# One table load at the last norm, sums of squares inside a projection, and stores and sample loads on GpSimd's queue

## The chip, the cores and the metric

The kernel runs on one core of a Trainium2 chip. A core has five engines, each with an instruction stream of its own that it works off in order: TensorE for matrix products (PE in the profile, with PEld for the load of a stationary operand), VectorE (DVE), ScalarE (ACT), GpSimd (POOL) and SyncE (SP), which here does nothing but issue DMA transfers. GpSimd can issue DMA transfers too. Engines wait for one another, and for transfers, through semaphores. The metric is device time in microseconds (us) of one execution; lower is better.

## What is computed

One inference step of a two-layer decoder for a prompt of 1024 tokens and for 8 sample tokens that share all weights. The model width is 1024. Layer 0's mixer is a gated recurrence (4 heads) beside attention into 256 memory tokens; layer 1's is stick-breaking attention beside the same kind of memory attention. Each layer has a SwiGLU network of width 2816, and an RMSNorm stands before and after each part:

```
def rmsnorm(x, g):
    return x * lax.rsqrt(jnp.mean(x * x, axis=-1, keepdims=True) + EPS) * g

def swiglu(h, w_gu, w_down):
    gate, up = jnp.split(h @ w_gu, 2, axis=-1)
    return (jax.nn.silu(gate) * up) @ w_down

for l in range(DEPTH):                 # DEPTH = 2
    hn = rmsnorm(h, g[0])
    mix = a_mixer(hn, ...) if l < N_A else b_mixer(hn, ...)     # N_A = 1
    h = h + rmsnorm(mix, g[1])
    h = h + rmsnorm(swiglu(rmsnorm(h, g[2]), w_gu[l], w_down[l]), g[3])
    if l == N_A - 1:                   # one K/V pair, shared by the layers behind it
        sb_k, sb_v = jnp.split(rmsnorm(h, g_kv) @ w_kv, 2, axis=-1)
```

A sample token attends to keys and values that come from DRAM: 256 past positions of the shared K/V, in pages that a table of page numbers points to, and 256 memory tokens per layer. Everything is float32.

## The kernel before

Activations lie with the model width on the partitions, in eight tiles of 128, and tokens along the free axis. The tokens go in two groups: g = 0 holds 512 prompt tokens, g = 1 the other 512 and the 8 sample tokens as eight last columns (520 in all, worked off as two pieces of 260). A product of two float32 operands is made from three products of rounded high and low parts, so every weight tile is fetched (L212, on SP's queue), rounded on ACT (L217) and its remainder taken on DVE (L218); the result `ws` holds four blocks of 128x128. Five raw tiles and five split tiles are in rotation. For the SwiGLU network's weights the same is done at L588, L621 and L623. PE multiplies at L231 (`proj`: one output tile, tag `mm`, two PSUM banks in rotation), L628 and L800.

The order of the work comes from generators. `weave` steps two or three of them in turn by given weights, which writes the program; a list scheduler then fixes each engine's order, and from there on every engine is in order. Places that matter here:

- `rstd_from` turns a tile of summed squares `st` into reciprocal roots. It splits it in two halves (`n`, L238 on ACT and L239 on DVE), lets PE add over the partitions with a matrix of ones (L279), and applies a logarithm (L280) and an exponential (L281) on ACT. A bank holds 512 columns, so in group 1 the loop goes round twice, for 512 columns and for the last 8, both times in the same PSUM bank `ns`, which exists once.
- `out_proj.finish` is the step behind an output projection: `rstd_from`, then `residual` for eight tiles (DVE L445 scales, L451 adds the stored residual rows that L432 fetched, L453 stores the new rows `hs` to DRAM, ACT L289 squares, DVE L290 sums), then a second `rstd_from` and `normed` (DVE L297).
- `mixer_b.heads` projects eight heads for layer 1's mixer; ACT L1490 takes a head's result from its PSUM bank. It is woven with `out_proj.finish` of the other group, twice: group 1 of layer 0 at about 930 us, and group 0 of layer 1 at about 1477 us.
- The last norm is `out_proj.finish` of group 1 in layer 1, at about 1965 us, woven with the SwiGLU network of group 0. That network's sigmoid (L646) and the norm's logarithm and exponential need different tables of ACT's activation unit, and a change of table is an instruction of its own, ACT_TABLE_LOAD, which the profile puts on the line of the activation behind it.
- The sample tokens of layer 1 (about 1520 to 1880 us) attend on DVE and ACT. `sample_scores` writes the eight queries to DRAM (`qd`, L1108), reads each back broadcast over the partitions (`b<-qd`, L1114), multiplies it into a tile of keys (L1116) and sums (L1119). The keys come by page from the shared K/V (`page_loader`, L1177, indirect DMA on GpSimd) or from the memory tokens (`mem_loader`, L1165, SP's queue). `sample_pv` scales values on ACT (L1141), and PE adds them up.

All DMAs but L1177's and those that sum gate and up weights ahead of time (L701, L703, `wsum`) are issued by SP, one after another.

Of the kernel before, what the change touches and what calls it, by code (L numbers as in the profile page):

```python
# [18 lines left out]
P = 128  # L19
# [4 lines left out]
def tile_decoder(  # L24
# [197 lines left out]

    def proj(g, W, k0, nk, m0, xt):
        w = split_w(W, k0, nk, m0)
        ps = mmp.tile([P, 2, 512], F32, tag="mm", name=nm("mm"))
        for k in range(nk):
            wh, wl = w[k]
            for wi, (wt, xi) in enumerate(((wh, 0), (wh, 1), (wl, 0))):
                for a in range(NPC[g]):
                    o = a * PW[g]  # L230
                    nc.tensor.matmul(  # L231
                        ps[:, a, : PW[g]], wt, xt[k][:, xi, o : o + PW[g]],
                        start=(k == 0 and wi == 0), stop=(k == nk - 1 and wi == 2),
                    )
        return ps

# [35 lines left out]
    def rstd_from(acc, n, inv, dst=None, bank=NS):  # L272
        r = acc if dst is None else dst
        parts = halves(acc[:, :n], *(npool.tile([P, WID], F32R, tag="n", name=nm("n"))[:, :n] for _ in range(2)))
        for o in range(0, n, 512):
            w = min(512, n - o)
            ps = bank()
            for i, p in enumerate(parts):
                nc.tensor.matmul(ps[:, :w], onesr, p[:, o : o + w], start=(i == 0), stop=(i == 1))  # L279
            nc.scalar.activation(r[:, o : o + w], ps[:, :w], AF.Ln, scale=inv, bias=epsb)  # L280
        nc.scalar.activation(r[:, :n], r[:, :n], AF.Exp, scale=-0.5)  # L281
        return r
# [139 lines left out]
    def residual(g, R, rstd, gc, store, acc=None, first=False, paced=False):  # L422
# [13 lines left out]
        for k in range(ND):  # L436
# [15 lines left out]
            if store:  # L452
                nc.sync.dma_start(hs[g][:, k, :n], R[k][:, :n])  # L453
            if acc is not None:
# [13 lines left out]
    class out_proj:  # L468
# [35 lines left out]
        def finish(self):  # L504
            g, l = self.g, self.l
            rstd = rstd_from(self.acc, NG[g], 1.0 / D)
            acc = small([P, WID], tag="st", bufs=3)
            yield from residual(g, self.R, rstd, lambda k: gcol(l, 1, k), not self.last, acc, l == 0, l == 1 and g == 0)
            r2 = rstd_from(acc, NG[g], 1.0 / D)
            yield  # L510
# [584 lines left out]

    def sample_scores(q, load, sc):
        qc = small([P, H * NB], tag="ss")
# [9 lines left out]
        qd = tc.dram_tile([NB, 512], F32, name=nm("qd"))  # L1107
        nc.sync.dma_start(qd, qt[:NB, :])  # L1108
        yield
        scv = sc.rearrange("p (k h b) -> p k h b", k=2, h=H)  # L1110
        for b in range(NB):
            kt = load(b)
            qb = B()
            nc.sync.dma_start(qb, qd[b].partition_broadcast(P))  # L1114
            with tc.issue_after(split[0].ins):
# [46 lines left out]
    def mem_loader(src, l):  # L1162
        def load(b):
            t = C()
            nc.sync.dma_start(t, src[l, b].rearrange("(k p) h d -> p k (h d)", p=P))  # L1165
            return t

        return load
# [16 lines left out]
    def mem_attn_sample(l, qm, xo):  # L1185
        HB = H * NB
        sc = small([P, 2 * HB], tag="sc", bufs=2)
        yield from sample_scores(qm, mem_loader(cache_mem_k, l), sc)
        yield
# [21 lines left out]

    def heads2(g, W, m0, xt, evac, alloc, out):
        for h in range(H):
            if h % 2 == 0:
                out.append(alloc())
            ps = proj(g, W, 0, ND, m0 + h * P, xt)
            evac(out[-1][:, h % 2, :], ps, g)
# [487 lines left out]
    class mixer_b:  # L1705
        def __init__(self, g, xt):
            self.g, self.xt, self.Qs, self.Qm = g, xt, [], []

        def heads(self):
            yield from heads2(self.g, w_in_b[0], 0, self.xt, scaled_evac, A, self.Qs)  # L1710
            yield from heads2(self.g, w_in_b[0], 4 * P, self.xt, scaled_evac, A, self.Qm)
# [164 lines left out]
    b0 = mixer_b(0, xb0)  # L1876
    weave((b0.heads(), 8), (o1.finish(), 17))
    b0.open(True)
# [18 lines left out]
    b1 = mixer_b(1, xb1)  # L1897
    weave((b1.heads(), 8), (o0.finish(), 17))
    b1.open()
# [52 lines left out]
```

## Time and profile before

| what | value |
| --- | --- |
| time, median of 3 runs | 2401.22 us (2400.32 to 2401.59) |
| the profiled execution's own time | 2400.42 us |
| its span, first to last instruction | 2398.7 us |
| PE busy | 2377.8 us, 99% |
| DVE, ACT, POOL busy | 71%, 55%, 5% |
| granted clock of TensorE | 0.999 |
| DMA | 357.60 MB in 515233 packets |

The profiled execution lies 0.80 us under the median of the three runs. Its own time is 1.7 us more than its span. An idle time in the profile is printed in brackets behind an instruction, with what released it. Waits of the queue engines (SPq, POOLq) are listed apart from those of the engines that compute.

### The profile page before, as it was taken

The page shows a single profiled execution, that of the slowest core. Times are in us where ns is not written, and L with a number is a line of the kernel's source. Part 1 is how long each engine was busy: PE and PEld are TensorE (multiplying, and loading weights), DVE is VectorE, ACT ScalarE, POOL GpSimd, SP SyncE. Part 2 cuts the span into 40 slices and gives each one's busy share as a digit, 9 for nine tenths or more (in the row PEclk, how much of TensorE's full clock was granted, in tenths as well). Part 3 has the DMA queues.
Part 4 walks back from the last instruction along what each step waited for, and adds up shares of the span by engine and source line. Part 5 has one row for each costly group of instructions (what it writes and reads, how often), then busy time and mean ns, then how long its engine had stood idle before and what let it go on. Part 6 is the DMA issues. An engine that isn't in the chain of part 4 may idle for free.

```text
span 2398.7 us, 42471 instructions
## 1 busy us (share of the span) xinstructions
PE 2377.8 (99%) x15962; PEld 2158.4 (90%) x15962; DVE 1710.1 (71%) x3197; ACT 1323.1 (55%) x2734; POOL 113.0 (5%) x187
## 2 busy tenths in 40 slices
PE   9999999999999999999999999999999999999998
PEld 7888989888889998999999989887778989999998
DVE  5867558766776677879566777877776779676866
ACT  4547544454574554667544554568557566554445
POOL 1001202101000000000001100111000000000000
PEclk9999999999999999999999999999999999999999
DMA  6454776677535447332668746544454354343442
GB/s 195 119 171 116 172 204 161 166 185 200 167 110 162 138 146 228 110 102 87 173 178 216 207 147 191 171 141 142 123 172 123 98 154 128 119 128 98 115 125 75
DMA packets 515233, 357.60 MB, mean 149 GB/s; under 512 B 20245, under 2 KB 463746, under 8 KB 515026
## 3 DMA queue, kind: packets, MB, share of 16 engines
q1 hardware_dynamic: 499154, 312.93, 44.1%
q0 software_dynamic: 15872, 41.95, 7.5%
q8 instruction: 126, 2.06, 0.4%
q14 instruction: 81, 0.66, 0.1%
HBM read 322.86 MB, written 65.49 MB: 162 GB/s over the span
## 4 chain that ended last, share of the span: by engine, by line
PE 93%; DVE 3%; ACT 2%; DMA 1%; issue 1%; SPq 0%; DVEq 0%; ACTq 0%
PE mm L231 42%; PE q L628 18%; PE q L800 12%; PE q L554 4%; PE mm L1253 2%; PE s L1434 1%; PE s L1069 1%; PE s L1050 1%; PE s L1614 1%; PE s L1657 1%; PE mm L986 1%; PE mm L1013 1%; PE q L832 1%; PE s L554 1%; PE s L1646 1%
## 5 line engine op out<-in xcount | busy, mean ns | idle before, releaser
L231 PE MATMUL mm<-x,ws 128*128 128x512 f32 (+1 forms) x5016 | 924.3, 342 | 4.1 <-ACT b L1640 2.2
L231 PEld LDWEIGHTS mm<-x,ws 128*128 128x128 f32 x5016 | 775.1, 188 | 115.5 <-ACT b L1640 2.6
L217 ACT CAST ws<-w 128x512 fp32r<-128x512 f32 x596 | 346.1, 584 | 396.9 <-PE mm L231 230.6
L218 DVE TENSOR_TENSOR ws<-w,ws 128x512 fp32r<-128x512 f32 x596 | 379.4, 644 | 225.0 <-ACT ws L217 217.0
L800 PE MATMUL q<-m,ws 128*128 128x260 f32 (+1 forms) x2496 | 303.9, 283 | 0.1
L800 PEld LDWEIGHTS q<-m,ws 128*128 128x128 f32 x2496 | 300.0, 188 | 0.9 <-ACT m L238 0.3
L628 PE MATMUL q<-y,ws 128*128 128x260 f32 (+1 forms) x1920 | 249.3, 284 | 0.0
L628 PEld LDWEIGHTS q<-y,ws 128*128 128x128 f32 x1920 | 237.7, 188 | 0.9 <-ACT q L640 0.2
L628 PE MATMUL q<-x,ws 128*128 128x260 f32 (+1 forms) x1668 | 219.8, 283 | 1.3 <-DVE ws L623 0.7
L628 PEld LDWEIGHTS q<-x,ws 128*128 128x128 f32 x1668 | 207.8, 188 | 2.2 <-DVE ws L623 1.1
L231 PE MATMUL mm<-m,ws 128*128 128x512 f32 x768 | 187.0, 397 | 0.0
L621 ACT CAST ws<-w 128x512 fp32r<-128x512 f32 x206 | 125.0, 619 | 97.1 <-PE q L800 30.7
L623 DVE TENSOR_TENSOR ws<-w,ws 128x512 fp32r<-128x512 f32 x206 | 139.2, 687 | 45.5 <-ACT ws L621 41.7
L231 PEld LDWEIGHTS mm<-m,ws 128*128 128x128 f32 x768 | 142.7, 188 | 32.0
L809 DVE TENSOR_TENSOR r<-r,q 128x260 f32<-128x260 f32 (+1 forms) x160 | 60.5, 419 | 48.7 <-PE q L800 48.3
L554 PE MATMUL q<-x,ws 128*128 128x260 f32 (+1 forms) x720 | 87.0, 282 | 0.0
L554 PEld LDWEIGHTS q<-x,ws 128*128 128x128 f32 x720 | 86.3, 188 | 0.2
L621 ACT CAST ws<-b 128x512 fp32r<-128x512 f32 x82 | 50.6, 620 | 42.4 <-PE q L800 13.4
L238 ACT CAST m<-t 128x512 fp32r<-128x512 f32 (+1 forms) x88 | 54.7, 621 | 33.3 <-DVE t L873 15.8
L239 DVE TENSOR_TENSOR m<-t,m 128x512 fp32r<-128x512 f32 (+1 forms) x88 | 60.7, 690 | 14.6 <-ACT m L238 13.7
L623 DVE TENSOR_TENSOR ws<-b,ws 128x512 fp32r<-128x512 f32 x82 | 56.3, 687 | 20.1 <-ACT ws L621 19.4
L290 DVE TENSOR_TENSOR st<-st,n 128x512 f32<-128x512 f32 (+1 forms) x91 | 62.1, 689 | 3.4 <-ACT n L289 1.9
(431 smaller groups left out, 3113.7 us busy)
## 6 DMA issues: line engine op xcount, KB each, us to landing
w<-in_w_gu SPq DMA_DIRECT2D x275, 256.0 KB, 3.3
w<-in_w_down SPq DMA_DIRECT2D x160, 256.0 KB, 3.0
wsum<-in_w_gu POOLq DMA_DIRECT2D x48, 512.0 KB, 6.3
w<-in_w_in_a SPq DMA_DIRECT2D x80, 256.0 KB, 3.3
w<-in_w_o SPq DMA_DIRECT2D x64, 256.0 KB, 3.0
w<-wsum SPq DMA_DIRECT2D x61, 256.0 KB, 3.6
b<-in_w_gu SPq DMA_DIRECT2D x39, 256.0 KB, 3.8
b<-wsum SPq DMA_DIRECT2D x39, 256.0 KB, 3.0
```

The costliest lines, as they stand in the source:

```text
L217: nc.scalar.copy(ws[:, 0, :n, :], raw[:, :n, :])
L218: split[0] = nc.vector.tensor_sub(ws[:, 1, :n, :], raw[:, :n, :], ws[:, 0, :n, :].bitcast(F32))
L231: nc.tensor.matmul(ps[:, a, : PW[g]], wt, xt[k][:, xi, o : o + PW[g]], start=(k == 0 and wi == 0), stop=(k == nk - 1 and wi == 2),)
L238: nc.scalar.copy(dst[0], src)
L239: nc.vector.tensor_sub(dst[1], src, dst[0].bitcast(F32))
L290: nc.vector.tensor_add(acc[:, :n], acc[:, :n], t[:, :n])
L554: ins = nc.tensor.matmul(pp[a][:, :h], wt, xt[k][:, xi, a * h : (a + 1) * h], start=(k == 0 and wi == 0), stop=(k == ND - 1 and wi == 2),)
L621: nc.scalar.copy(w[:, 0, :], src)
L623: split[0] = nc.vector.tensor_sub(w[:, 1, :], src, w[:, 0, :].bitcast(F32))
L628: nc.tensor.matmul(ps[:, :h], w[:, wj, k * P : (k + 1) * P], x[:, xi, :], start=(first and k == 0 and wi == 0), stop=(k == 3 and wi == 2), ...
L800: nc.tensor.matmul(pp[a][:, :h], wt, mids[k][:, xi, a * h : (a + 1) * h], start=(k == 0 and wi == 0), stop=(k == nf - 1 and wi == 2),)
L809: nc.vector.tensor_add(d, d, pp[a][:, :h])
```

## The change

It has five parts.

1. In `rstd_from` the last 8 columns of group 1 get a PSUM bank of another pool (`S()`), and all matrix products with ones are written ahead of the logarithms.
2. `heads2` and `mixer_b.heads` take a generator. Within the first head's projection, when three of eight steps are still to come, the projection calls its first step; the generator is `out_proj.finish`, whose first step is `rstd_from` and the first tile of `residual`.
3. In the last `out_proj.finish` the table with logarithm and exponential is loaded by an instruction of its own, tied behind the last sigmoid-times-gate activation `act[0]`.
4. The stores of residual rows `hs` are issued by GpSimd, except those of group 0 in layer 0's mixer: 32 of 40.
5. In layer 1 the sample's query stores (2), query broadcasts (16) and memory loads (16) are issued by GpSimd. Layer 0's stay on SP.

Together 66 DMAs go from SP's queue to GpSimd's.

```diff
-    def proj(g, W, k0, nk, m0, xt):
+    def proj(g, W, k0, nk, m0, xt, mid=None):
...
+            if mid and k == nk - 3:
+                mid()
         return ps
...
     def rstd_from(acc, n, inv, dst=None, bank=NS):
         r = acc if dst is None else dst
         parts = halves(acc[:, :n], *(npool.tile([P, WID], F32R, tag="n", name=nm("n"))[:, :n] for _ in range(2)))
+        pieces = []
         for o in range(0, n, 512):
             w = min(512, n - o)
-            ps = bank()
+            ps = S() if o else bank()
             for i, p in enumerate(parts):
                 nc.tensor.matmul(ps[:, :w], onesr, p[:, o : o + w], start=(i == 0), stop=(i == 1))
-            nc.scalar.activation(r[:, o : o + w], ps[:, :w], AF.Ln, scale=inv, bias=epsb)
+            pieces.append((r[:, o : o + w], ps[:, :w]))
+        for d, ps in pieces:
+            nc.scalar.activation(d, ps, AF.Ln, scale=inv, bias=epsb)
         nc.scalar.activation(r[:, :n], r[:, :n], AF.Exp, scale=-0.5)
         return r
...
             if store:
-                nc.sync.dma_start(hs[g][:, k, :n], R[k][:, :n])
+                (nc.sync if first and not g else nc.gpsimd).dma_start(hs[g][:, k, :n], R[k][:, :n])
...
             yield from residual(g, self.R, rstd, lambda k: gcol(l, 1, k), not self.last, acc, l == 0, l == 1 and g == 0)
+            if self.last:
+                with tc.issue_after(act[0].ins):
+                    nc.scalar.preload_act_table_set("natural_log_exp_and_others")
             r2 = rstd_from(acc, NG[g], 1.0 / D)
...
-    def sample_scores(q, load, sc):
+    def sample_scores(q, load, sc, l=1):
+        queue = nc.gpsimd if l else nc.sync
...
-        nc.sync.dma_start(qd, qt[:NB, :])
+        queue.dma_start(qd, qt[:NB, :])
...
-            nc.sync.dma_start(qb, qd[b].partition_broadcast(P))
+            queue.dma_start(qb, qd[b].partition_broadcast(P))
...
     def mem_loader(src, l):
         def load(b):
             t = C()
-            nc.sync.dma_start(t, src[l, b].rearrange("(k p) h d -> p k (h d)", p=P))
+            (nc.gpsimd if l else nc.sync).dma_start(t, src[l, b].rearrange("(k p) h d -> p k (h d)", p=P))
...
-    def heads2(g, W, m0, xt, evac, alloc, out):
+    def heads2(g, W, m0, xt, evac, alloc, out, mid=None):
         for h in range(H):
...
-            ps = proj(g, W, 0, ND, m0 + h * P, xt)
+            ps = proj(g, W, 0, ND, m0 + h * P, xt, None if h else mid)
...
-        def heads(self):
-            yield from heads2(self.g, w_in_b[0], 0, self.xt, scaled_evac, A, self.Qs)
+        def heads(self, mid):
+            yield from heads2(self.g, w_in_b[0], 0, self.xt, scaled_evac, A, self.Qs, lambda: next(mid))
...
-    weave((b1.heads(), 8), (o0.finish(), 17))
+    fin = o0.finish()
+    weave((b1.heads(fin), 8), (fin, 17))
```

The weave of `b0.heads` with `o1.finish` is changed in the same way. Lines of the changed kernel lie 2 to 9 further down: L279 becomes L282, L280 L285, L281 L286, L238 L240, L453 L458, L646 L654, L1108 L1117, L1114 L1123, L1165 L1174, L1177 L1186; L231 and L217 stay, and the new table load is L516.

How the order of the instructions moves, at three places. Names with an underscore and a number are single tiles.

TensorE at about 1477 us, the first projected head of group 1 in layer 1 (`mm`) with the ones (L279, then L282) of the first `rstd_from` in `out_proj.finish`. Before:

```order
L231 MATMUL mm_16536<-x_16510,ws_16533 128x260 x6
L231 MATMUL mm_16536<-x_16514,ws_16533 128x260 x6
L231 MATMUL mm_16536<-x_16518,ws_16533 128x260 x6
L231 MATMUL mm_16536<-x_16522,ws_16533 128x260 x6
L279 MATMUL ns_16590<-n_16586,onesr 128x512
L279 MATMUL ns_16590<-n_16587,onesr 128x512
L231 MATMUL mm_16630<-x_16455,ws_16622 128x260 x6
L231 MATMUL mm_16630<-x_16498,ws_16622 128x260 x6
```

and with the change:

```order
L231 MATMUL mm_16536<-x_16510,ws_16533 128x260 x6
L231 MATMUL mm_16536<-x_16514,ws_16533 128x260 x6
L282 MATMUL ns_16577<-n_16573,onesr 128x512
L282 MATMUL ns_16577<-n_16574,onesr 128x512
L231 MATMUL mm_16536<-x_16518,ws_16533 128x260 x6
L231 MATMUL mm_16536<-x_16522,ws_16533 128x260 x6
L231 MATMUL mm_16636<-x_16455,ws_16628 128x260 x6
L231 MATMUL mm_16636<-x_16498,ws_16628 128x260 x6
```

The rows with `x6` are one of the eight steps of a head each. The two products with ones stood behind the first head's eight steps, ahead of the second head; now they stand behind its sixth step, 12 matmuls of 260 columns earlier.

ScalarE at the last norm, around its first logarithm (L280, then L285); `m`, `q`, `t` and `ws` belong to the SwiGLU network of group 0 beside it. Before:

```order
L636 ACTIVATE q_21355<-q_21353 128x256
L621 CAST ws_21453<-b_21451 128x512
L621 CAST ws_21472<-w_21470 128x512
L621 CAST ws_21493<-b_21491 128x512
L621 CAST ws_21520<-w_21518 128x512
L280 ACT_TABLE_LOAD
L280 ACTIVATE st_21035<-ns_21419,epsb 128x512
L238 CAST m_21412<-t_21307 128x512
L280 ACTIVATE st_21035<-ns_21423,epsb 128x8
L640 ACTIVATE q_21356<-q_21355 128x256
L281 ACT_TABLE_LOAD
L281 ACTIVATE st_21035<-st_21035 128x520
```

and with the change:

```order
L676 ACTIVATE t_21307<-t_21328 128x256
L644 ACTIVATE q_21355<-q_21353 128x256
L516 ACT_TABLE_LOAD
L629 CAST ws_21454<-b_21452 128x512
L629 CAST ws_21473<-w_21471 128x512
L629 CAST ws_21494<-b_21492 128x512
L629 CAST ws_21521<-w_21519 128x512
L285 ACTIVATE st_21035<-ns_21420,epsb 128x512
L240 CAST m_21412<-t_21307 128x512
L285 ACTIVATE st_21035<-s_21423,epsb 128x8
L648 ACTIVATE q_21356<-q_21355 128x256
L286 ACTIVATE st_21035<-st_21035 128x520
```

The table load that stood ahead of the first logarithm stands right behind the activation L644 (L636 before), ahead of four casts, and the one ahead of the exponential (L281, then L286) is gone.

The queues at the beginning of the sample tokens' stick-breaking attention, at about 1523 us. Before, the query store and the broadcasts stood on SP among the weight loads, and GpSimd held the page gathers alone:

```order
L1678 DMA a_17669<-vsc_155 128x2x512
L1108 DMA qd_17151<-b_17149 8x512
L212 DMA w_17389<-in_w_gu 128x4x128
L1114 DMA b_17198<-qd_17151 128x512
L212 DMA w_17453<-in_w_gu 128x4x128
L212 DMA w_17458<-in_w_gu 128x4x128
L212 DMA w_17518<-in_w_gu 128x4x128
L1114 DMA b_17253<-qd_17151 128x512
L212 DMA w_17523<-in_w_gu 128x4x128
L1114 DMA b_17358<-qd_17151 128x512
```

and with the change, on GpSimd:

```order
L458 DMA hs_144<-m_15471 128x512 x2
L1186 DMA c_17195<-in_cache_sb_k,pidx 128x512
L1117 DMA qd_17151<-b_17149 8x512
L1186 DMA c_17195<-in_cache_sb_k,pidx 128x512
L1186 DMA c_17250<-in_cache_sb_k,pidx 128x512 x2
L1123 DMA b_17198<-qd_17151 128x512
L1123 DMA b_17253<-qd_17151 128x512
L1123 DMA b_17358<-qd_17151 128x512
L1186 DMA c_17355<-in_cache_sb_k,pidx 128x512 x2
L1186 DMA c_17426<-in_cache_sb_k,pidx 128x512 x2
L1123 DMA b_17429<-qd_17151 128x512
```

The query store and the broadcasts stand in one row with the gathers: three gathers lie between the store and the first broadcast, and the broadcasts of the second and third sample row are written right behind the first.

More of the change, by code (lines that the diff above doesn't have):

```diff
@@ L1187, in mem_attn_sample @@
         sc = small([P, 2 * HB], tag="sc", bufs=2)
-        yield from sample_scores(qm, mem_loader(cache_mem_k, l), sc)
+        yield from sample_scores(qm, mem_loader(cache_mem_k, l), sc, l)
         yield
@@ L1876, in tile_decoder @@
     b0 = mixer_b(0, xb0)
-    weave((b0.heads(), 8), (o1.finish(), 17))
+    fin = o1.finish()
+    weave((b0.heads(fin), 8), (fin, 17))
     b0.open(True)
```

## The prediction

> **What bounds the kernel now.** I read the page's engine shares and its chain first, then PE's busy time by stage, and last the time line of every stage that the change touches.
>
> ```profile
> PE 2377.8 (99%) x15962; PEld 2158.4 (90%) x15962; DVE 1710.1 (71%) x3197; ACT 1323.1 (55%) x2734; POOL 113.0 (5%) x187
> ...
> PE 93%; DVE 3%; ACT 2%; DMA 1%; issue 1%; SPq 0%; DVEq 0%; ACTq 0%
> ```
>
> PE is the bound: it is busy for 99% of the span and holds 93% of the chain. The change adds and removes no matrix product, so it can win only where PE stands still. A table by stage (window, its length, then busy time of PE, PEld, DVE, ACT, POOL, granted clock, DMA share, GB/s) shows where that is:
>
> ```profile
> 820.00:1000.00 180.00, 179.95 (x1129) 159.51 (x1128) 136.43 (x243) 98.09 (x177) 0.00 (x0) 1.00 0.54 165
> ...
> 1460.00:1505.00 45.00, 43.10 (x331) 40.95 (x330) 37.94 (x64) 26.16 (x46) 0.00 (x0) 1.00 0.65 206
> 1505.00:1700.00 195.00, 195.00 (x993) 158.44 (x992) 146.86 (x229) 128.67 (x274) 30.87 (x28) 1.00 0.47 142
> 1700.00:1880.00 180.00, 177.75 (x844) 143.28 (x842) 126.36 (x208) 104.96 (x241) 0.00 (x0) 1.00 0.47 141
> ...
> 1950.00:2000.00 50.00, 48.45 (x372) 46.06 (x371) 45.19 (x81) 39.70 (x74) 0.00 (x0) 1.00 0.51 151
> ```
>
> Length less PE's busy time is PE's idle time: 0.05 us with the first woven projection of heads (820 to 1000), 1.90 with the second (1460 to 1505), 0.00 in the sample tokens' page attention, 2.25 in their memory attention (1700 to 1880), 1.55 around the last norm. Together 5.75 us: that is the ceiling of the gain, 0.24% of the time. What a measurement of this kernel can tell from no change is about 0.2%, 4.8 us.
>
> **Ones inside the heads' projection (part 2).** The second place, in order of time:
>
> ```profile
> 1474.63 0.69 DVE L239 TENSOR_TENSOR n<-st,n 128x512 fp32r<-128x512 f32 x1 [0.69 <-ACT n L238]
> ...
> 1477.06 0.63 PE L279 MATMUL ns<-n,onesr 128*128 128x512 f32 x2
> 1477.26 0.61 ACT L1490 ACTIVATE a<-mm 128x520 f32<-128x520 f32 x1 [2.67 <-PE mm L231]
> ...
> 1477.53 9.72 PE L231 MATMUL mm<-x,ws 128*128 128x260 f32 x80
> ...
> 1478.48 0.63 ACT L281 ACTIVATE st<-st 128x512 f32<-128x512 f32 x1
> 1479.15 1.41 DVE L445 SCALAR_TENSOR_TENSOR m<-m,par,st 128x512 f32<-128x512 f32 x2 [3.82 <-ACT st L281]
> ...
> 1487.28 0.68 DVE L218 TENSOR_TENSOR ws<-w,ws 128x512 fp32r<-128x512 f32 x1
> ...
> 1488.02 2.68 PE L231 MATMUL mm<-x,ws 128*128 128x260 f32 x20 [0.77 <-DVE ws L218]
> ...
> 1490.59 0.63 ACT L289 ACTIVATE n<-m 128x512 f32<-128x512 f32 x1 [3.10 <-DVE m L451]
> ...
> 1491.76 6.38 PE L231 MATMUL mm<-x,ws 128*128 128x260 f32 x51 [1.06 <-ACT a L1490]
> ```
>
> The halves are ready at 1474.63 + 0.69 = 1475.32, yet the ones run at 1477.06, behind the first head's last steps. DVE stands for 3.82 us and starts L445 at 1479.15. From there it is the stage's late engine: the remainder L218 that PE needs comes at 1487.28 (PE stands 0.77), and ACT waits 3.10 for DVE's L451 before the square L289, behind which L1490 frees PE's bank late (PE stands 1.06). A matmul of 260 columns takes 9.72 / 80 = 0.12 us, so the ones move 12 x 0.12 = 1.46 us forward to 1475.60, which is after the halves are ready: they wait for nothing. L1490 (0.61) no longer stands between ones and logarithm. With 0.63 for the ones, then 0.69 and 0.63 plus gaps for logarithm and exponential, L445 starts at about 1477.65, 1.5 us earlier. 1.5 exceeds each of the two waits, 0.77 and 1.06, and the second starts from a DVE queue already moved. Bounds: 0 if the 1.5 us are eaten on the way (ACT's casts before 1481 stand on weights in flight), 1.90 if all idle time goes. I take **-1.8**, near the upper end, since 1.5 covers either wait. What is late next is ACT's cast of the next weights. At the first place PE has 0.05 us idle, so nothing can be won: **0**.
>
> **Own bank and one table load (parts 1 and 3).** The last norm:
>
> ```profile
> 1968.05 0.62 ACT L621 CAST ws<-w 128x512 fp32r<-128x512 f32 x1 [0.74 <-PE q L628]
> ...
> 1968.69 1.28 ACT L280 ACT_TABLE_LOAD   x1
> ...
> 1971.71 1.28 ACT L281 ACT_TABLE_LOAD   x1
> ...
> 1973.66 1.28 ACT L646 ACT_TABLE_LOAD   x1
> ...
> 1974.96 0.38 ACT L646 ACTIVATE t<-q 128x256 f32<-128x256 f32 x1
> ...
> 1975.39 1.67 PE L628 MATMUL q<-x,ws 128*128 128x256 f32 x12 [0.52 <-ACT t L646]
> ...
> 1978.51 2.63 PE L628 MATMUL q<-a,ws 128*128 128x256 f32 x20 [0.27 <-DVE ws L623]
> ...
> 1988.16 1.44 PE L628 MATMUL q<-x,ws 128*128 128x256 f32 x10 [0.59 <-DVE ws L623]
> ```
>
> Three loads of 1.28 us stand within 6.3 us of ACT's time; two remain. The first moves ahead of four casts L621, which come 1.28 us later. Their cover is the rotation of five split tiles: the last of them stood 0.74 us for a tile that PE had yet to free, so weights were split ahead as far as the rotation allows, and the real delay is 1.28 - 0.74 = 0.54 us. Without that cover PE would wait 1.28. From there ACT saves the load at 1971.71: L646, which released PE at 1975.39, comes some 1.1 us sooner by the sequence of ACT's durations (1.28 less the cast that now stands ahead of its load and the small gaps). PE's wait of 0.52 goes, and the 0.27 at 1978.51 with it, since the casts behind move too. The 0.59 at 1988.16 lies ten us on and may stay. Bounds: 0, and 1.55 with all of the idle time. I take **-1.2**, the idle time less a part of the 0.59. The own bank takes the wait of the 8-column ones for the logarithm out of the row; PE's share in that is inside the same 1.55.
>
> The row gives 1.28 us for a switch of tables and shows no draining behind it: L646 starts 0.02 us after its load ends. The Trainium skill, page "ScalarE: Activation LUTs", section "What ACT_TABLE_LOAD costs", sets a switch at about 2.66 us, a load of 1.283 and a drain of 1.38. The trace agrees on the load alone; by the page the removed switch would be worth 2.66 us of ACT, yet PE's idle time would still cap the stage at 1.55, so the sum would be 0.35 better.
>
> **Sample loads on GpSimd's queue (part 5).** The chain of waits for the memory attention:
>
> ```profile
> 1722.01 0.47 SPq L1114
> ...
> 1722.52 6.99 DMA c<-in_cache_mem_k
> ...
> 1732.72 0.46 SPq L212
> ...
> 1733.27 5.25 DMA b<-qd
> ...
> 1738.61 0.13 DVE c L1116
> ...
> 1740.47 0.64 ACT b L1640
> ...
> 1741.19 5.79 PE mm L231 x24
> ```
>
> SP issued the third tile of keys only at 1722.5 and the fourth broadcast at 1733.2, because weight loads that wait for a free tile stand between them in SP's row. The broadcast lands at 1738.52, DVE's product L1116 runs then, and the work behind it on DVE and ACT releases PE at 1741.19, 2.25 us late; that is the whole idle time of the stage. On GpSimd no weight load stands between these transfers. The chain puts both down to SP's own row and to no slot, so both come several us sooner: **-2.2**, with bounds 0 (a broadcast still in flight) and 2.25.
>
> A new wait stands against it at the start of the page attention, where the broadcast has to pass gathers. These rows give prices (ns least, median, most) and the place:
>
> ```profile
> L703 POOL DMA_DIRECT2D wsum<-in_w_gu x16: 560/590/1312, 223.3 to 1304.9; - x16
> ...
> L1177 POOL DMA_INDIRECT c<-in_cache_sb_k,pidx x16: 940/1149/1756, 1341.6 to 1581.5; - x16
> ...
> L453 SPq DMA_DIRECT2D hs<-m x24: 319/338/484, 334.3 to 1495.4; - x24
> ...
> 1523.28 0.31 SPq L1108 DMA_DIRECT2D qd<-b  x1
> ...
> 1528.90 1.22 DVE L1116 TENSOR_TENSOR c<-c,b 128x1024 f32<-128x1024 f32 x1
> ...
> 1533.10 0.95 POOL L1177 DMA_INDIRECT c<-in_cache_sb_k,pidx  x1 [0.31 <-issue]
> ...
> 1540.64 5.81 PE L231 MATMUL mm<-x,ws 128*128 128x512 f32 x24
> ```
>
> Behind the query store at 1523.28 come 0.59 for its issue and three gathers of 1.15 with 0.31 between: the first broadcast is issued at about 1528.3 and, with the 5.25 us of the row above, lands at 1533.5. DVE's L1116 started at 1528.90, so DVE stands about 4.6 us. Behind it in DVE's row wait remainders L218 and the reading of a bank that PE needs again at 1540.64. Moving that reading by 4.6 us still leaves it ahead of 1540.64, and the next broadcasts, written right behind the first, arrive sooner than before. Bounds: 0 and about 1.5, if the remainders fall behind as well. I take **+0.3**. The moved loads that follow cost 0.59 of GpSimd each instead of SP's; GpSimd is busy for 5%, and nothing but these transfers is in its row there.
>
> **Row stores (part 4).** 32 stores cost GpSimd 0.59 each for SP's 0.34. They are read back hundreds of us later, and in the first stage named PE is idle for 0.05: **0**. Behind the last eight stands the first page gather, due at 1528.90 and issued by 1500.
>
> **Sum.** -1.8 - 1.2 - 2.2 + 0.3 = -4.9 us on the profiled execution's own 2400.42, or 2395.5. That execution lies 0.8 under the median of the runs shown, so on the median's scale it is 2401.2 - 4.9 = **2396.3**.
>
> **Rivals.**
> *The sample loads win nothing.* For it: they are still in order, a load with its broadcast, and a key tile's load waits for DVE's L1119 wherever it is issued. Then the 2.2 falls away and the page attention's new wait is 1 or more: 2401.2 - 3.0 + 1.0 = 2399.2. Against it: the chain names SP's queue.
> *The waits of the heads and of the last norm only move.* DVE is busy for 84% of the window from 1460 (37.94 of 45.00) and 90% of the one from 1950; a split tile that is late elsewhere takes over, and half of -3.0 is kept: 2401.2 - 1.5 - 1.9 = 2397.8. Both of these lie within 0.2%.
> *Slower: DVE held behind GpSimd's row.* GpSimd's loads wait for slots in order, and a broadcast stands behind a load that waits:
>
> ```profile
> SPq L1165 <- DVE sc L1119: 17.9, 5, 7.2
> ```
>
> SP's loads did so 5 times, 3.6 us each (17.9 in all). If in GpSimd's row each makes a broadcast late and DVE holds back PE's banks as at 1741.19, 5 x 2.25 = 11 us come in for the 2.2 lost: 2401.2 - 3.0 + 11 = 2409. It decides from the third such wait on, 3 x 2.25 = 6.8 against the 4.9. Against it: in GpSimd's row the next broadcast often stands ahead of the load (the order above), and the page attention's DVE waits cost PE 0.00 before.
> The Trainium skill, page "SBUF — State Buffer", section "SBUF: two separate sides", says that GpSimd cannot write its descriptors while certain DVE instructions hold a shared port. By that each moved transfer would wait out a DVE instruction, an estimate of 1.2 us with L1116's duration, and this rival would be likelier. The row of L703 speaks against it: a median of 590 ns beside a DVE that is busy for 71%, with 1312 as the most.
>
> **How the numbers follow.** My forecast, all three stalls gone or nearly so: 0.55, from 2394.5 to 2397.5, and 0.45 of it falls beyond the 4.8 us (under 2396.4), 0.10 short of it. The sample loads win nothing: 0.15; waits only move: 0.12, with 0.02 beyond the bound by other small gains; slower: 0.18, with 0.02 that ends within 0.2%. So faster 0.47, same 0.37, slower 0.16. The range leaves out the far part of the slower case (0.13) and under 0.06 below: 2394.5, the ceiling's 2395.5 and one us for waits outside the touched stages, to 2403.0.
>
> **What would show it.** Right: 11 table loads in place of 12; the ones at 1475.6 on the old clock and no wait of PE for L218 or L1490 behind them; PE's idle time under 0.4 us in the windows of the heads and the memory attention, and under 0.6 at the last norm; a DVE wait of 4 to 5 us for the first `b<-qd`. Wrong: PE idle in the page attention (0.00 before), longer DVE waits for `qd` and keys in the memory attention with PE standing behind them, or DVE instructions that grow longer while GpSimd issues.

## The result

The changed kernel took 2395.54 us (median of 15 runs, 2393.47 to 2396.44) where the kernel before took 2401.28 (15 runs beside them): a ratio of 0.9975 with a 95% interval of 0.9968 to 0.9981, or 5.7 us less. The forecast was 2396.3 and 4.9 us less. The sum held; most of its terms did not. One of the six executions of page_sp_w13, an experiment further down, ran at a granted clock of 0.851 and took 2562.19 us; it is left out of that kernel's median and ratio. The page of the changed kernel, engine shares first:

```profile
PE 2376.1 (99%) x15962; PEld 2158.2 (90%) x15962; DVE 1710.2 (71%) x3197; ACT 1319.8 (55%) x2733; POOL 153.6 (6%) x253
```

The table by stage, with the windows that the prediction used (the changed kernel runs about 1 us ahead in the first two, falls to 0.6 us behind in the page attention, and is 2 to 5 us ahead from the end of the memory attention on):

```profile
820.00:1000.00 180.00, 179.95 (x1130) 159.82 (x1129) 136.84 (x243) 97.61 (x177) 8.72 (x16) 1.00 0.54 165
...
1460.00:1505.00 45.00, 43.09 (x332) 40.93 (x331) 38.72 (x65) 26.46 (x46) 7.08 (x9) 1.00 0.69 208
1505.00:1700.00 195.00, 194.46 (x982) 156.78 (x981) 144.13 (x225) 125.28 (x270) 39.43 (x40) 1.00 0.48 146
1700.00:1880.00 180.00, 180.00 (x857) 145.27 (x856) 128.86 (x215) 107.06 (x246) 16.56 (x25) 1.00 0.46 141
...
1950.00:2000.00 50.00, 49.77 (x403) 48.76 (x402) 47.61 (x87) 39.65 (x75) 0.00 (x0) 1.00 0.55 165
```

PE's idle time went from 2.25 to 0.00 us in the memory attention and from 1.55 to 0.23 at the last norm. In the heads' stage it is 1.91 where it was 1.90, and the page attention has 0.54 where it had none.

Both programs issue the same 15962 matrix products, so the start of the n-th one in either trace says by how much a stretch became shorter (-) or longer (+), whether PE's time there is shown as idle or as busy. In us, stretches on the clock of the kernel before, the changed kernel in the first row and the experiments of the next section below it; one profiled execution each:

| kernel | to 720 | 720-1000 | 1000-1200 | 1200-1460 | 1460-1505 heads | 1505-1700 pages | 1700-1950 memory | 1950-1995 last norm | behind |
| --- | --- | --- | --- | --- | --- | --- | --- | --- | --- |
| changed | -0.50 | -0.21 | +0.51 | -0.67 | -0.03 | +1.58 | -2.66 | -3.10 | +0.25 |
| norm_off | -0.79 | +0.05 | +0.35 | -0.01 | +0.05 | +2.21 | -2.30 | +0.01 | +0.26 |
| no_preload | -2.06 | -0.25 | +0.43 | -0.66 | +0.05 | +2.49 | -2.36 | -0.07 | +0.73 |
| one_bank | -0.32 | +0.03 | +0.56 | 0.00 | -0.02 | +1.81 | -2.41 | -2.89 | +0.50 |
| part5_off | -1.16 | -0.22 | +0.27 | -0.68 | +0.01 | 0.00 | -0.88 | -3.13 | +0.85 |
| page_sp | -1.68 | -0.24 | -0.19 | -0.68 | +0.06 | 0.00 | -2.21 | -3.10 | +0.47 |
| no_mid | -0.80 | -0.34 | -0.21 | -0.68 | +0.57 | +1.55 | -2.65 | -3.12 | +0.66 |
| stores_sp | -0.66 | -0.21 | +0.20 | -0.70 | +0.01 | +1.39 | -2.65 | -3.10 | +1.10 |
| w15 | -0.85 | -0.29 | -0.21 | -0.68 | -1.33 | +1.23 | -2.29 | -3.13 | +0.90 |
| page_sp_w15 | +0.56 | -0.25 | +0.06 | -0.65 | -1.30 | 0.00 | -2.35 | -3.10 | +0.74 |
| page_sp_w13 | -0.66 | +0.15 | +0.11 | -0.65 | -2.36 | -0.01 | -2.52 | -3.10 | +1.34 |

No kernel differs from the one before in the first 720 us, so the spread of the first column (-2.06 to +0.56) is what one execution differs from another by. Where the code in them is the same, the columns of the heads and of the last norm repeat within 0.1 us, that of the memory within 0.5; the pages' column spreads by 1.3 (1.23 to 2.49) and the one behind by 1.1. The changed kernel's row sums to -4.85; the rest of the 5.8 us between the two spans lies in front of the first product (0.1) and behind the last (0.8).

**Heads.** The time line of the changed kernel, engine by engine:

```profile
1473.62 0.69 DVE L241 TENSOR_TENSOR n<-st,n 128x512 fp32r<-128x512 f32 x1 [0.69 <-ACT n L240]
...
1474.61 0.63 PE L282 MATMUL ns<-n,onesr 128*128 128x512 f32 x2
...
1476.66 1.41 DVE L450 SCALAR_TENSOR_TENSOR m<-m,par,st 128x512 f32<-128x512 f32 x2 [2.35 <-ACT st L286]
...
1486.67 0.68 DVE L218 TENSOR_TENSOR ws<-w,ws 128x512 fp32r<-128x512 f32 x1
...
1487.40 2.66 PE L231 MATMUL mm<-x,ws 128*128 128x260 f32 x20 [1.16 <-DVE ws L218]
...
1490.76 5.66 PE L231 MATMUL mm<-x,ws 128*128 128x260 f32 x45 [0.69 <-ACT a L1499]
```

The halves are ready at 1474.31, 1.01 us earlier than before (the lead of the whole program here), and the ones, L282, follow 0.30 us behind them, where it was 1.74 before. (They stand behind the sixth of the first head's eight steps, so two steps are still to come, not three as the description of part 2 has it.) L450 starts 1476.66 - 1474.31 = 2.35 us behind the halves where L445 started 3.83 behind them: the promised 1.5 us. Yet L218 comes at 1486.67, which on the same footing is 0.4 us later than before, and PE's two waits are 1.16 and 0.69 in place of 0.77 and 1.06. DVE worked without a gap in between: it had more in front of L218. Its order in the two programs, from the first L445 (L450) to that L218:

```
before:  L445 x2  L451 x2  L445 x2  L290  L451 x2  L445  L290  L451  L290                                   L218
changed: L450 x2  L456 x2  L450 x2  L295  L456 x2  L450  L295  L456  L295  L450  L295  L456                 L218
```

Thirteen instructions were ahead of it, now there are sixteen: the first step of the woven generator is taken out of turn, so `weave` is one step further whenever it comes to a later head, and one more tile of the residual (0.74 + 0.68 + 0.68 = 2.1 us by the rows of this stage) stands ahead of the weights. The L218 in question belongs to the third head: PE stops 80 products behind the ones (92 in the changed kernel, where 12 of the first head follow them), and a head has 48. The expectation for w15 calls it the second.

**Last norm.** ACT's table loads and what released PE before:

```profile
1963.53 1.28 ACT L516 ACT_TABLE_LOAD   x1
...
1969.62 1.28 ACT L654 ACT_TABLE_LOAD   x1
...
1970.72 3.00 PE L636 MATMUL q<-x,ws 128*128 128x256 f32 x24
1970.91 0.39 ACT L654 ACTIVATE t<-q 128x256 f32<-128x256 f32 x1
...
1973.55 3.00 PE L636 MATMUL q<-a,ws 128*128 128x256 f32 x24
```

From the first logarithm on there are two loads in place of three, and none of the four waits of PE that the profile before showed there; PE goes through 24 products where it had stopped after 12.

**Page attention.** What stands in GpSimd's row ahead of the first broadcast, and who waits:

```profile
1522.76 0.56 POOL L1117 DMA_DIRECT2D qd<-b  x1 [27.12 <-DVE b L1115]
...
1523.63 1.46 POOL L1186 DMA_INDIRECT c<-in_cache_sb_k,pidx  x1 [0.30 <-issue]
...
1525.40 1.05 POOL L1186 DMA_INDIRECT c<-in_cache_sb_k,pidx  x1 [0.30 <-issue]
...
1526.75 0.94 POOL L1186 DMA_INDIRECT c<-in_cache_sb_k,pidx  x1 [0.30 <-issue]
...
1527.69 1.70 POOL L1123 DMA_DIRECT2D b<-qd  x3
...
1533.69 1.23 DVE L1125 TENSOR_TENSOR c<-c,b 128x1024 f32<-128x1024 f32 x1 [5.74 <-DMA b<-qd]
```

The broadcast is issued 4.93 us behind the query store and is there some 6.0 later; DVE stands for 5.74. PE does not stop at 1540, where it needs the bank that DVE reads. It stops later, at 1546.01 and 1595.15, behind ACT and DVE work that runs late:

```profile
PE s L1655 <- ACT t L263: 0.2, 1, 0.2
PE mm L231 <- DVE m L241: 0.3, 1, 0.3
```

### The profile page after: what moved, and what is told of

The parts are those of the page before. It is cut to its first block, busy times and chain, and to the rows that moved or that the text cites. A ratio compares the mean times of both kernels' runs of the same rounds, so it can differ in the third digit from the quotient of the medians.

```text
span 2392.9 us, 42508 instructions
## 1 busy us (share of the span) xinstructions
PE 2376.1 (99%) x15962; PEld 2158.2 (90%) x15962; DVE 1710.2 (71%) x3197; ACT 1319.8 (55%) x2733; POOL 153.6 (6%) x253
## 5 line engine op out<-in xcount | busy, mean ns | idle before, releaser
L231 PE MATMUL mm<-x,ws 128*128 128x512 f32 (+1 forms) x5016 | 923.6, 342 | 2.0 <-DVE ws L218 1.2
L231 PEld LDWEIGHTS mm<-x,ws 128*128 128x128 f32 x5016 | 774.5, 188 | 113.6 <-DVE ws L218 1.4
L217 ACT CAST ws<-w 128x512 fp32r<-128x512 f32 x596 | 345.7, 584 | 391.1 <-PE mm L231 226.5
L218 DVE TENSOR_TENSOR ws<-w,ws 128x512 fp32r<-128x512 f32 x596 | 380.1, 645 | 226.9 <-ACT ws L217 218.6
L636 PE MATMUL q<-y,ws 128*128 128x260 f32 (+1 forms) x1920 | 249.4, 284 | 0.4 <-ACT q L644 0.4
L636 PEld LDWEIGHTS q<-y,ws 128*128 128x128 f32 x1920 | 237.7, 188 | 1.2 <-ACT q L644 0.6
L636 PE MATMUL q<-x,ws 128*128 128x260 f32 (+1 forms) x1668 | 219.1, 283 | 0.2 <-DVE ws L631 0.2
L636 PEld LDWEIGHTS q<-x,ws 128*128 128x128 f32 x1668 | 207.7, 188 | 0.7 <-DVE ws L631 0.3
L231 PE MATMUL mm<-m,ws 128*128 128x512 f32 x768 | 187.4, 397 | 0.3 <-DVE m L241 0.3
L231 PEld LDWEIGHTS mm<-m,ws 128*128 128x128 f32 x768 | 142.5, 188 | 32.9 <-DVE m L241 0.6
L240 ACT CAST m<-t 128x512 fp32r<-128x512 f32 (+1 forms) x88 | 54.7, 621 | 35.4 <-DVE t L881 17.2
```

Of the source, the lines that this page charges most:

```text
L217: nc.scalar.copy(ws[:, 0, :n, :], raw[:, :n, :])
L218: split[0] = nc.vector.tensor_sub(ws[:, 1, :n, :], raw[:, :n, :], ws[:, 0, :n, :].bitcast(F32))
L231: nc.tensor.matmul(ps[:, a, : PW[g]], wt, xt[k][:, xi, o : o + PW[g]], start=(k == 0 and wi == 0), stop=(k == nk - 1 and wi == 2),)
L240: nc.scalar.copy(dst[0], src)
L636: nc.tensor.matmul(ps[:, :h], w[:, wj, k * P : (k + 1) * P], x[:, xi, :], start=(first and k == 0 and wi == 0), stop=(k == 3 and wi == 2), ...
```

## The experiments

Each kernel is the changed one with the edit shown. Ratios are to the kernel before, run beside it on the same chip, with 95% intervals; the changed kernel's own is 0.9975.

**The page attention's loads back on SP (page_sp).**

```diff
-        yield from sample_scores(Qs, page_loader(cache_sb_k), zb)
+        yield from sample_scores(Qs, page_loader(cache_sb_k), zb, 0)
```

> The changed kernel, with the query store and broadcasts of the page attention back on SP's queue; those of the memory attention stay on GpSimd. Theory (the first broadcast behind three gathers holds DVE 5.7 us and costs PE about 1.6 us between 1540 and 1600): 1.6 us less than the changed kernel's 2395.5, so about 2393.9; PE idle in the page attention back from 0.54 to 0.0, and no DVE wait over 1 us for the first broadcast. Rival (the 1.6 us come from the changed order of DVE and ACT there, not from the late broadcast): 2395.5, with idle time left in that stage.

Measured: 2393.01 us, ratio 0.9972 (0.9961 to 0.9984). The trace settles it where the interval can't: the stage loses its +1.58 to 0.00, and DVE does not wait for the first broadcast, which SP issues 1.76 us behind the store.

```profile
1520.56 0.31 SPq L1117 DMA_DIRECT2D qd<-b  x1
...
1522.32 0.34 SPq L1123 DMA_DIRECT2D b<-qd  x1
...
1526.18 1.22 DVE L1125 TENSOR_TENSOR c<-c,b 128x1024 f32<-128x1024 f32 x1
```

So having the query store and the broadcasts behind GpSimd's gathers is the cause; the memory attention keeps -2.21 of its -2.66.

**All sample loads back on SP (part5_off).**

```diff
-            (nc.gpsimd if l else nc.sync).dma_start(t, src[l, b].rearrange("(k p) h d -> p k (h d)", p=P))
+            nc.sync.dma_start(t, src[l, b].rearrange("(k p) h d -> p k (h d)", p=P))
...
-        yield from sample_scores(qm, mem_loader(cache_mem_k, l), sc, l)
+        yield from sample_scores(qm, mem_loader(cache_mem_k, l), sc, 0)
```

and the edit of page_sp.

> The changed kernel without part 5: all sample loads of layer 1 on SP again. Theory (part 5 wins 2.5 us in the memory attention and loses 1.6 in the page attention, nothing elsewhere): 0.9 us more than the changed kernel, about 2396.4; PE stands about 2.2 us once between 1735 and 1745 again, and the last norm keeps its gain. Rival (a relieved SP queue is also what wins at the last norm, 3.1 us): about 2399.5, with PE's waits there back.

Measured: 2395.95 us, ratio 0.9985 (0.9976 to 0.9994). The last norm keeps its whole gain (-3.13), so SP's relief from the sample loads has no part in it. The wait in the memory attention is back, though smaller than in the kernel before:

```profile
1738.67 5.80 PE L231 MATMUL mm<-x,ws 128*128 128x512 f32 x24 [1.50 <-ACT b L1649]
```

Part 5 is worth -2.66 + 0.88 = -1.8 there and +1.6 in the page attention: next to nothing together by the traces. The times would allow more: the ratio is 0.0010 above the changed kernel's, some 2.4 us, with intervals that overlap from 0.9976 to 0.9981.

**The last norm without parts 1 and 3 (norm_off), without part 3 (no_preload), without part 1 (one_bank).** The first joins the edits of the other two.

```diff
-            if self.last:
-                with tc.issue_after(act[0].ins):
-                    nc.scalar.preload_act_table_set("natural_log_exp_and_others")
```

```diff
-            ps = S() if o else bank()
+            ps = bank()
...
-            pieces.append((r[:, o : o + w], ps[:, :w]))
-        for d, ps in pieces:
-            nc.scalar.activation(d, ps, AF.Ln, scale=inv, bias=epsb)
+            nc.scalar.activation(r[:, o : o + w], ps[:, :w], AF.Ln, scale=inv, bias=epsb)
```

> The changed kernel without parts 1 and 3: one bank for both pieces of the ones, and no table load of its own. Theory (parts 1 and 3 win about 3.1 us at the last norm): about 2398.6, 12 table loads, PE idle of 1.4 to 1.6 us around 1955 to 1995. Rival (the gain there is from the moved loads and stores): 2395.5 to 2396, with PE idle under 0.5 us there.

> The changed kernel without part 3 alone: no table load of its own; the last 8 columns keep their own bank and the ones stay ahead of the logarithms. Theory (the loads are what delays the last norm; the activation between the logarithms and the exponential needs another table): the three loads around the last norm come back and most of the 3.1 us: about 2398. Rival (the bank and the order of the logarithms are what wins, the loads lie beside other work): about 2396.

> The changed kernel without part 1 alone: one bank for both pieces of the ones, logarithm between them; the table load of its own stays. Theory (loads): 2395.5 to 2396, PE idle at the last norm under 0.6 us. Rival (bank): about 2398, with PE waiting for the logarithm in front of the ones of the last 8 columns.

Measured: norm_off 2398.89 us, ratio 0.9995 (0.9986 to 1.0004); no_preload 2398.82, 0.9991 (0.9982 to 1.0001); one_bank 2396.87, 0.9986 (0.9977 to 0.9995). Without the table load of its own all three loads and all waits of PE are back at the last norm, although the bank is there:

```profile
1966.34 1.28 ACT L285 ACT_TABLE_LOAD   x1
...
1969.29 1.28 ACT L286 ACT_TABLE_LOAD   x1
...
1971.24 1.28 ACT L651 ACT_TABLE_LOAD   x1
...
1972.97 1.68 PE L633 MATMUL q<-x,ws 128*128 128x256 f32 x12 [0.52 <-ACT t L651]
```

The separate load (part 3) is worth 2.90 to 3.03 us there, the bank 0.21. The rows also correct the theory for no_preload: the activation between the logarithms and the exponential (a copy times -1, L645 there, L648 in the changed kernel) has no load in front of it. The loads stand ahead of the first logarithm and ahead of the exponential, and in the changed kernel the one load at L516 serves both. Part 3 drops one load and moves another ahead of the casts; no run separates the two. The bank wins elsewhere too: from 1200 to 1460 the kernels with one bank (norm_off, one_bank) have -0.01 and 0.00 where all with two have -0.65 to -0.70, and from 720 to 1000 they have +0.05 and +0.03 where those with two have -0.21 to -0.34, page_sp_w13 (+0.15) excepted. The other norms of group 1 lie there. Their wait was in the profile before, in who waited for L280, as a wait of PE's weight load and not of PE:

```profile
  PEld ns L279: 1.7, 6
```

Six waits for the logarithm in front of the 8-column ones, 0.28 us each, which the changed kernel does not have; kernels with one bank have them. Five of the six lie in the three stretches named. Part 1 so wins 0.24 + 0.67 + 0.21 = 1.1 us, the first term less surely than the others. The expectation for one_bank, 2395.5 to 2396, missed that; the rival for it, that the bank carries the last norm, is not borne out.

**Part 2 taken out (no_mid), and DVE's order restored (w15).**

```diff
-            yield from heads2(self.g, w_in_b[0], 0, self.xt, scaled_evac, A, self.Qs, lambda: next(mid))
+            yield from heads2(self.g, w_in_b[0], 0, self.xt, scaled_evac, A, self.Qs)
```

```diff
-    weave((b1.heads(fin), 8), (fin, 17))
+    weave((b1.heads(fin), 8), (fin, 15))
```

> The changed kernel without part 2: the ones behind the first head's projection again. Theory (DVE's new order takes back what the earlier ones win, so part 2 is worth 0): 2395.5 within 0.5 us, PE idle in the heads' stage at 1.9 us as with part 2, and DVE's remainder L218 behind 13 residual instructions in place of 16. Rival (part 2 wins 1 to 2 us that the profile does not show): 2396.5 to 2397.5.

> The changed kernel with one number changed: in the second weave the steps behind the output projection get weight 15 in place of 17, which puts DVE's remainder L218 for the second head behind 13 residual instructions, as before the change, with the ones still early. Theory (DVE's order took back the gain of part 2): PE's two waits at about 1487 and 1490 shrink from 1.85 us together to under 0.5 and the time falls by 1.5 to 2 us, to about 2393.8. Rival (the weights' DMA or ACT's casts hold the stage): waits of 1.5 us or more are left and the time is 2395.5.

Measured: no_mid 2395.14 us, ratio 0.9980 (0.9971 to 0.9989); w15 2393.74, 0.9974 (0.9965 to 0.9983). Taking part 2 out costs the heads' stage 0.60 us of the changed kernel's time and the interval sees nothing, so in the changed kernel it is worth about half a us, where theory had 0. L218 stands behind 13 residual instructions again, as expected, but PE's idle time in the stage is 2.34 us and not 1.9. The stage is 0.57 longer than in the kernel before, although DVE works in the same order: the first cast of the weights behind the ones waits 1.29 us for its transfer, where it was 0.70. Why that transfer came later is open.

```profile
1478.37 0.62 ACT L217 CAST ws<-w 128x512 fp32r<-128x512 f32 x1 [1.29 <-DMA w<-in_w_in_b]
...
1486.43 2.67 PE L231 MATMUL mm<-x,ws 128*128 128x260 f32 x20 [1.20 <-DVE ws L218]
```

With the weight 15, L218 stands behind 13 residual instructions again while the ones stay early, and PE's wait for it is gone; one wait is left:

```profile
1475.49 1.41 DVE L450 SCALAR_TENSOR_TENSOR m<-m,par,st 128x512 f32<-128x512 f32 x2 [2.35 <-ACT st L286]
...
1483.63 0.68 DVE L218 TENSOR_TENSOR ws<-w,ws 128x512 fp32r<-128x512 f32 x1
...
1488.11 6.38 PE L231 MATMUL mm<-x,ws 128*128 128x260 f32 x51 [0.62 <-ACT a L1499]
```

The stage is 1.33 us shorter than before, with the waits at 0.62 together against 1.85 (under 0.5 was expected). DVE's order was what took part 2's gain: w15 and no_mid have the same order on DVE up to 1495 us and differ in the place of the ones, and their stages differ by 1.90 us. This is read from the traces alone; the ratio of w15 (0.9974) does not differ from the changed kernel's (0.9975) by more than the noise.

**The row stores back on SP (stores_sp).**

```diff
-                (nc.sync if first and not g else nc.gpsimd).dma_start(hs[g][:, k, :n], R[k][:, :n])
+                nc.sync.dma_start(hs[g][:, k, :n], R[k][:, :n])
```

> The changed kernel without part 4: all row stores on SP's queue again. Theory (PE is fully busy where the stores are, so they are worth 0): 2395.5 within 0.6 us. Rival (the 0.5 us that the changed kernel is ahead between 1400 and 1460 come from them): 2396.0 to 2396.5 with PE idle there.

Measured: 2394.78 us, ratio 0.9976 (0.9967 to 0.9986). The stretch from 1200 to 1460 keeps its -0.70: the stores had no part in that, nor in the last norm's -3.10. Part 4 is worth nothing that can be measured.

**Repairs together (page_sp_w15, page_sp_w13).** The edit of page_sp with weight 15, and with weight 13.

> The changed kernel with the page attention's query store and broadcasts on SP and weight 15 in place of 17 in the second weave: both single repairs together. If the two stages are independent, their gains add: PE's waits as in each alone, and 1.6 + 1.3 = 2.9 us less than the changed kernel, a ratio to the kernel before of about 0.9964. If the page attention starts in another state because the heads end earlier, one of the two gains is smaller and the ratio is 0.997 or more.

> As before, with weight 13: DVE's remainders for the heads stand ahead of still more of the residual. If the one wait that weight 15 leaves (0.62 us, ACT's reading of a head's bank behind a square that waits for DVE) comes from residual instructions as well, it falls below 0.3 and the ratio to the kernel before is about 0.996. Rival: the last residual tile then comes late for what follows (the second sum of squares and the first gate weights), and a new wait of PE of 0.5 us or more stands between 1490 and 1530.

Measured: page_sp_w15 2393.10 us, ratio 0.9967 (0.9954 to 0.9979); page_sp_w13 2391.32, ratio 0.9959 (0.9946 to 0.9972). The stages are independent: -1.30 in the heads and 0.00 in the pages, as in each alone. With 13 the last wait of the heads goes too, and the stage is 2.36 us shorter than before; PE's busy time in the window around it:

```profile
1455.00:1505.00 50.00, 49.93 (x392) 48.18 (x392) 41.54 (x71) 28.86 (x50) 9.61 (x12) 1.00 0.71 223
```

Of the feared wait behind it nothing shows up to 1700. page_sp_w13 is the fastest kernel here: its ratio lies 0.0016 under the changed kernel's, some 4 us; the two intervals still overlap between 0.9968 and 0.9972, and the stages add the -2.33 and -1.59 to it.

## Why the prediction came out, and where it was wrong

**Heads, -1.8: wrong.** Measured -0.03. The step that failed is "1.5 exceeds each of the two waits, 0.77 and 1.06", taken with DVE's order as it was. The ones came early and L450 1.5 us earlier, as worked out, but the out-of-turn step put one more residual tile, 2.1 us, ahead of L218. w15, which keeps the ones early and restores the 13 instructions, wins 1.33 against the kernel before and 1.90 against no_mid, so the promised 1.8 was there to be had with the order unchanged. Weight 13 wins 2.36, more than the 1.90 that I took for the ceiling. The rival "waits only move" was right here, and the bound 0 "if the 1.5 us are eaten on the way" was too, by DVE's row and not by ACT's casts as the prediction had it.

**Last norm, -1.2: right in its mechanism, mis-sized.** Measured -3.10. The separate load is what wins (no_preload), and the cover of the four casts held. The term was capped at the window's idle time, 1.55, and that was too low a ceiling. PE's rows before show why:

```profile
1973.28 1.59 PE L628 MATMUL q<-x,ws 128*128 128x256 f32 x12
...
1977.22 1.02 PE L628 MATMUL q<-a,ws 128*128 128x256 f32 x4 [0.16 <-ACT ws L621]
```

A row of 24 products at 1970.72 in the changed kernel is 3.00 us long, yet the next row starts 2.83 later: the end that the profile models for the last product lies some 0.17 us behind the point from which the next one could run. Idle time is printed from that end on. So the products' starts tell more. Without a stop, products of 256 columns start 0.118 us apart. The one at 1975.39 starts 0.796 us behind the one ahead of it, and the next 0.223 behind that: 0.68 + 0.10 = 0.78 us are lost where 0.52 is printed. The five stops of the stage cost 0.78, 0.42, 0.28, 0.54 and 0.85 us, 2.88 together, where the profile prints 0.52, 0.16, nothing, 0.27 and 0.59. Each cost about 0.27 us more than its idle time, and the sum is close to the 2.90 to 3.03 of part 3. The heads' two waits, printed as 0.77 and 1.06, cost 1.03 and 1.33 in the same way, which is the 2.36 that weight 13 won.

On ACT, the last of the four casts comes 0.5 us later once the program's lead of 2.1 us is taken off (0.54 was worked out), and L654 starts 8.08 us behind the start of the activation L676, where L646 stood 10.01 behind L668: 1.93 sooner, and not 1.1. The moved load also fills the 0.74 us that ACT had waited for a tile.

The rule of the Trainium skill on the page "ScalarE: Activation LUTs", section "What ACT_TABLE_LOAD costs", which gives a drain of 1.38 us beside the load, is not borne out by a row: in the changed kernel too the activation L654 starts 0.01 us after its load's end (1969.62 + 1.28 to 1970.91), and the load starts 0.02 us after the cast ahead of it ends (1968.99 + 0.61 to 1969.62).

**Memory attention, -2.2: right.** Measured -2.66 with the stop's hidden part, 2.21 to 2.65 in the other kernels that have it. Only about 1.8 of it hangs on the queue, since part5_off, on SP, stood 1.50 in place of 2.25.

**Page attention, +0.3: too low.** Measured +1.58. The broadcast is issued 4.93 us behind the store, nearly as worked out (5.0). DVE's wait is 5.74 us and not 4.6, because the broadcast took 6.0 to land in place of 5.25 and DVE was ready for it 0.4 sooner behind the store. The reading of the bank does stay ahead of 1540, where PE does not stop. The step that failed is to end the count there: the late row of DVE reaches PE further on, through ACT at 1546.01 and DVE at 1595.15, and in two shorter stops between, with 0.5 us of idle time and the rest in what each stop costs beyond it. The upper bound of 1.5 was the better value.

**Own bank, nothing outside the last norm: wrong.** The sum has no term for it there, and it wins about 0.9 us in the other norms of group 1. The step that failed is reading PE's idle time alone (0.05 us in 820 to 1000): weight loads that wait, PEld, delay products without leaving PE idle in the table.

**Row stores, 0: right.** The prices were near: GpSimd issued a store in 0.54 us (0.59 taken), a broadcast in 0.57.

**Slower, by loads in GpSimd's row: did not come.** DVE's waits for broadcasts between 1500 and 1880 are two, 5.7 us for the first of the page attention and 1.5 for the first of the memory attention:

```profile
DVE c L1125 <- DMA b<-qd: 7.2, 2, 5.7
```

In the kernel before, DVE waited there 2.6 us for broadcasts and 5.9 us for memory tiles; for those tiles it no longer waits.

Nor did the transfers wait out DVE's instructions, as the prediction's estimate by the Trainium skill, page "SBUF — State Buffer", section "SBUF: two separate sides", had it: the 16 broadcasts that GpSimd issued took 0.54 to 0.61 us each, with DVE busy for 144.13 of 195.00 and 128.86 of 180.00 us beside them. Which of DVE's instructions there hold the port that the page means, no row shows, so this is no test of the page's rule. The gathers' own issue took 0.94 to 2.77 us; what makes it vary is not shown.

```profile
L1123 POOL DMA_DIRECT2D b<-qd x16: 537/567/606, 1527.7 to 1768.7; - x16
```

So that the time came out within 0.8 us of the forecast is luck in large part: misses of opposite sign met, 1.8 too much for the heads and 1.3 too little lost in the pages against 1.9 too little for the last norm, 0.9 for the bank and 0.5 for the memory attention.

What stays open: why PE's wait in the memory attention is 1.50 in part5_off and 2.25 in the kernel before, with the same chain of loads ahead of it. Its transfers took less time, the broadcast 4.73 us in place of 5.25 and the tile of keys 6.84 in place of 6.99, but why is not shown:

```profile
1731.28 4.73 DMA b<-qd
```

Open too are 0.57 us of no_mid's heads, and the part of the gain between 0 and 720 us, which no edit touches and which differs from one execution to the next.

## What to carry to other kernels

An edit that only takes a step out of turn in a woven program moves every step behind it: read the order of the engine that is late, instruction by instruction, before costing what becomes ready earlier. PE's printed idle time is no ceiling for what its waits cost; compare starts of the same product in two traces, and read the waits of its weight loads beside those of its products. A transfer that others wait for should not share an in-order queue with slow ones issued ahead of it: moving loads off a crowded queue paid in one stage and was lost again in another, by three gathers.

## What the runs showed that was not expected

A stop of PE cost about 0.27 us more than the idle time that the profile prints (0.78 for 0.52, 1.03 for 0.77): some 0.16 us because idle time is counted from the modelled end of the product ahead, and 0.10 because the second product behind a stop starts 0.22 us behind the first in place of 0.12. Six waits of 0.28 us of a weight load, in front of products of 8 columns, are gone with the own bank; the stretches in which five of them lie became 1.1 us shorter, though PE's table shows no idle time for most of them.
